# Three attention value blocks moved in TensorE's order, and smaller first loads of x, in a two-layer decoder trunk

## The chip, the cores and the metric

The kernel runs on one core of a Trainium2 chip. The metric is the device time of one execution in microseconds (us). A core has five engines with queues of their own: PE (TensorE, the matmuls; its weight loads appear as PEld), DVE (VectorE), ACT (ScalarE), POOL (GpSimd) and SP (SyncE, which here issues the DMAs). They wait for one another through semaphores.

## The reference

One sequence of 256 tokens, 1024 wide, goes through two layers and a last RMSNorm. In each layer three token mixers read the same normalised input, each is multiplied by a gate, and their sum goes through `w_out`; then comes an MLP with a squared ReLU.

```python
p = h @ w_in            # queries, keys, values and gates of all three mixers
merged = (sigmoid(g_mla)  * (o_mla  @ w_branch_mla)     # causal attention, 8 heads
        + sigmoid(g_moba) * (o_moba @ w_branch_moba)    # 256 tokens are one block: causal attention, 8 heads
        + sigmoid(g_ret)  * (o_ret  @ w_branch_ret))    # retention with decay, 4 heads
x = x + merged @ w_out
x = x + square(relu(h2 @ w_mlp_up)) @ w_mlp_down
```

An attention head computes scores `q k^T`, a softmax over the causal part, and `p v`, 64 wide ("values" below).

## The kernel before

**Numbers.** A matrix is split into a high and a low part, and a product is made of three matmuls (`three`, L228 to L230): high times high, low times high, high times low. Weights arrive by DMA (L192, tile `raw`), ACT makes the high part (`whi`, L207) and DVE the low one (`wlo`, L209).

**Stages of a layer.** Projections of the normalised input for MLA and MoBA; then, in program order, the MLA gate (gmla), the MoBA gate (gmoba), the MLA branch matmul (bmla), the projections for retention (rqk, rv, rg), the MoBA branch (bmoba), the retention gate and branch, `w_out` and the MLP. The list `prog` holds these units, and `at(slot, step)` hangs smaller steps behind one of them: scores, transposes, values, ropes.

**One attention.** `attention()` serves both. For each head: scores (MLA's in `mla_score`; MoBA's four heads at a time in `together`, L478), the row maximum on DVE (L492, L495), its negative times the scale on DVE (L498), the exponential on ACT (L501), the reciprocal of the sum (L504) and the division on DVE (two instructions of L506), three PE transposes into `ps_pt` (L512, `turned`) and a copy to `probT` by ACT. `values(h0)` multiplies the values of four heads: sixteen matmuls that use 64 columns of the array (L540 with 256 moving columns, L542 with 128) into a tile `po`, which ACT and DVE then split into high and low (L249; `omlah`, `omlal`, `omobah`, `omobal`).

**The order of the work.** A scheduler places each engine's instructions by a simulated timeline, so a step may come out later or earlier than written. Where the order is to be fixed, `in_a_row(...)` turns the scheduler off for PE: the matmuls of all its jobs stand one behind the other, and what the other engines do with them follows. The rows concerned:

- In MLA `values(0)` (heads 0 to 3) and `values(4)` are handed on (L551) to the row of MoBA's first four score heads (L563). In layer 0 the scheduler nevertheless put six full matmuls between the two blocks of values; in layer 1 they stand together. In the text "V" is a block of values, "S" the scores of four heads, "full matmul" one of L228 to L230 (128 x 512).
- MoBA's `values(0)` stand ahead of its second four score heads (L564), and `values(4)` behind retention's scores (L1051, tile `ps_r`, `moba_last`).
- `turned` of MoBA's heads is hung on later slots (L565 to L567).

**Rope.** In layer 0, four pairs of heads of MoBA are rotated on POOL (`rope_turned`, L443 and L446): a DMA swaps quarters of the partitions into `qkoth`, POOL multiplies that and the original by tables and adds them. For retention, DVE does it, with one product on POOL.

**First loads.** `begin` (L617 ff.) issues the first weight tiles, and x comes in eight chunks of 128 KB, one for each step k of the first projection (`start`, matmuls at L739 to L750): chunks 2 and 3 in one DMA, chunks 4 to 7 in another, among the weight tiles `b0mq` 1 to 7 of 464 KB each (L632 to L639).

Of the kernel before, what the change touches and what calls it, by code (L numbers as in the profile page):

```python
# [19 lines left out]
KD = D // P  # L20
# [117 lines left out]
def trunk(ctx: ExitStack, tc: tile.TileContext, gx, wts, consts, gfin, gn, xtok, out):  # L138


    nc = tc.nc
# [10 lines left out]
    X = [GX[:, G_END:].rearrange("p (k s) -> p k s", k=4), cp.tile([P, 4, S], F32, name="x1")]  # L152
    x = gx[:, G_END:].rearrange("p (k s) -> p k s", k=KD)
# [34 lines left out]
    def transfer(key, raw, queue=nc.sync, parts=None):  # L188
        offset, n, c = where[key]
        sz = n * c  # L190
        for a, b in parts or ((0, sz),):
            queue.dma_start(  # L192
                raw[:, a:b], bass.AP(tensor=wts.tensor, offset=wts.offset + offset + a, ap=[[sz, P], [1, b - a]])
            )
# [20 lines left out]
    def acc_tile(name="acc"):  # L215
        return ps.tile([P, 512], F32, name=name, tag="acc", bufs=4)

    def misc_tile(name="misc"):
        return ps.tile([P, 512], F32, name=name, tag="misc", bufs=4)
# [18 lines left out]
    def small(name):  # L238
        return sb.tile([P, 8], F32, name=name, tag="st", bufs=12)
# [8 lines left out]
    def split_plain(src, hi, lo):  # L248
        return nc.scalar.activation(hi, src, AF.Copy), nc.vector.tensor_sub(lo, src, hi.bitcast(F32))  # L249
# [212 lines left out]
    def in_a_row(*jobs):  # L462


        with tc.manual_schedule(engines={mybir.EngineType.PE}):
            rest = [job() for job in jobs]
        for job in rest:
            job()
# [11 lines left out]
    def attention_head(score, scale):  # L480


        got = {}

        def scores(s_ps=None):
            if s_ps is None:
                s_ps = misc_tile("ps_s")
                score(s_ps[:, 0:P], slice(0, P), slice(0, P))
                score(s_ps[:, P : 3 * P], slice(P, S), slice(0, S))
            p = sb.tile([P, 3 * P], F32, name="prob", bufs=4)  # L490
            m = small("smx")
            nc.vector.tensor_tensor_reduce(  # L492
                p[:, 0:P], s_ps[:, 0:P], mask[:, P : 2 * P], 1.0, NEG_INF, ALU.add, ALU.max, m[:, 0:1]
            )
            nc.vector.tensor_tensor_reduce(  # L495
                p[:, P : 3 * P], s_ps[:, P : 3 * P], mask, 1.0, NEG_INF, ALU.add, ALU.max, m[:, 1:2]
            )
            nc.vector.tensor_scalar(m[:, 2:4], m[:, 0:2], -scale, None, op0=ALU.mult)  # L498
            spans = ((0, P), (P, 3 * P))
            for i, (a, b) in enumerate(spans):  # L500
                nc.scalar.activation(  # L501
                    p[:, a:b], p[:, a:b], AF.Exp, bias=m[:, 2 + i : 3 + i], scale=scale, accum_out=m[:, 4 + i : 5 + i]
                )
            nc.vector.reciprocal(m[:, 6:8], m[:, 4:6])  # L504
            for i, (a, b) in enumerate(spans):
                nc.vector.tensor_scalar(p[:, a:b], p[:, a:b], m[:, 6 + i : 7 + i], None, op0=ALU.mult)  # L506
            got["p"] = p

        def turn():
            pt = misc_tile("ps_pt")  # L510
            for i, src in enumerate((0, P, 2 * P)):
                nc.tensor.transpose(pt[:, P * i : P * i + P], got["p"][:, src : src + P], ident)  # L512
            pT = sb.tile([P, 3 * P], F32, name="probT", bufs=8)
            nc.scalar.activation(pT, pt[:, : 3 * P], AF.Copy)
            return pT

        return scores, turn

    def attention(oT, score, vs, scale, first, group=None, former=None):

        pT = {}

        def turned(h, turn):
            pT[h] = turn()

        def values(h0):


            o, v = acc_tile("po"), vs()
            for h in (h0 + 2, h0):
                cs = slice(S * (h - h0) // 2, S * (h - h0) // 2 + S)
                for i in range(2):
                    for j in (1, 0):
                        vh = v[i][:, VD * (h + j) : VD * (h + j) + VD]
                        dst = o[64 * j : 64 * j + 64, cs]
                        if i == 0:
                            nc.tensor.matmul(dst, vh, pT[h + j][:, 0:S], start=True, stop=False)  # L540
                        else:
                            nc.tensor.matmul(dst[:, P:S], vh, pT[h + j][:, S : 3 * P], start=False, stop=True)  # L542
            dst = (part[:, h0 // 2 : h0 // 2 + 2, :].rearrange("p k s -> p (k s)") for part in oT)
            return lambda: split_plain(o, *dst)

        heads = [attention_head(lambda o, qs, ks, h=h: score(h, o, qs, ks), scale) for h in range(8)]
        if group is None:
            for h, (scores, turn) in enumerate(heads):
                at(first + h, scores)
                at(first + h + 2, lambda h=h, turn=turn: turned(h, turn))  # L550
            return [lambda: values(0), lambda: values(4)]  # L551

        def four(h0):
            banks = group(h0)

            def rest():
                for h, bank in enumerate(banks, h0):
                    heads[h][0](bank)

            return rest  # L560


        at(first, lambda: in_a_row(*former, lambda: four(0)))  # L563
        at(first + GAP, lambda: in_a_row(lambda: values(0), lambda: four(4)))  # L564
        for i in range(2):  # L565
            for h in range(4):
                at(first + GAP * i + 3 + h // 2, lambda h=4 * i + h: turned(h, heads[h][1]))  # L567
        return lambda: values(4)

    def gates(l, key, xn):  # L570

# [43 lines left out]
    def begin(key, tag=None, bufs=None, queue=nc.sync, parts=None):  # L615
        if tag:
            started[key] = sb.tile([P, 512 if tag == "w2k" else 1024], F32, name="raw0", tag=tag, bufs=bufs)  # L617
        else:
            started[key] = wp.tile([P, 1024], F32, name="raw", bufs=RAW)
        transfer(key, started[key], queue, parts)  # L620
# [8 lines left out]
    xn = Normed(G_ATT, 0)  # L629
    xrows = [w2k("xrow") for _ in range(2 * NT)]  # L630
    begin((0, "b0mq", 1), "t4", T4, parts=((0, 416), (416, 928)))
    nc.sync.dma_start(X[0][:, 2:4, :], x[:, 2:4, :])  # L632
    begin((0, "b0mq", 2), "t4", T4)
    begin((0, "b0mq", 3), "t4", T4)
    nc.sync.dma_start(X[1], x[:, 4:8, :])
    begin((0, "b0mq", 4), "t4", T4)
    for k in range(5, KD):
        begin((0, "b0mq", k))
    for q in range(2 * NT):  # L639
        nc.sync.dma_start(xrows[q], xtok[:, q // 2, 512 * (q % 2) : 512 * (q % 2) + 512])  # L640
    begin((0, "mk", 0, 0))
# [14 lines left out]
    def at(slot, step):  # L656
        steps.setdefault(slot, []).append(step)

    def slot(key, j):
        return [k for k, _ in prog].index((key, j))  # L660
# [9 lines left out]
    def layer(l, xn, before):  # L670
# [219 lines left out]
        first = slot("mv", 3)  # L890
        at(first, lambda: omlaT.extend((t4("omlah"), t4("omlal"))))

        def mla_score(h, o, qs, ks):
            nc.tensor.matmul(o, mla["Q"][:, h, qs], mla["K"][:, h, ks], start=True, stop=True)  # L894

        mla_last = attention(omlaT, mla_score, lambda: mla["v"], QKD**-0.5, first)


# [15 lines left out]
        first = slot("gmoba1", 1)  # L914
        at(first, lambda: omobaT.extend((t4("omobah"), t4("omobal"))))

        def moba_scores(h0):
# [5 lines left out]
            return banks  # L923

        moba_last = attention(omobaT, None, lambda: mqkv["mv"], MB_D**-0.5, first, moba_scores, mla_last)


# [14 lines left out]
        rT, or_ps, aT, rg, oret = [], [], {}, {}, []  # L942
# [105 lines left out]
                merged_turn(0, i - 1)  # L1048

        branch(l, "bret", oretT, th_ret, merged, between)  # L1050
        at(slot("rg", 1), lambda: in_a_row(ret_scores, moba_last))  # L1051
        for h in range(RT_H):
            at(slot("rg", 3), lambda h=h: ret_values(h))
        at(slot("rg", 3), group_norm)
# [218 lines left out]
    for l in range(L):  # L1273
        xn, before = layer(l, xn, before)
# [6 lines left out]
GAP = 8  # L1281
T4 = 8
# [81 lines left out]
```

## Time and profile before

| | |
|---|---|
| median of three runs | 833.33 us (833.25 to 833.34) |
| the profiled execution | 833.55 us |
| its span on the core | 831.8 us |
| DVE busy | 588.3 us (71%) |
| ACT busy | 484.1 us (58%) |
| POOL busy | 91.0 us (11%) |
| HBM read | 150.98 MB |

The span runs from the first instruction to the last; 833.55 - 831.8 = 1.75 us lie around it. In the timeline a row gives the start, the time from the first start to the last end, the engine, the line, the operation, output and inputs, the shape, and how many instructions it holds. Matmuls are pipelined, so their durations overlap: what counts on PE is the distance from one start to the next.

### The profile page before, as it was taken

What the parts mean: (1) busy time and instruction counts of PE and PEld (TensorE: products, weight loads), DVE (VectorE), ACT (ScalarE), POOL (GpSimd) and SP (SyncE); (2) the same over time, 40 slices, a digit from 0 to 9 for tenths busy, and PEclk for the clock granted to TensorE, in tenths of its full rate; (3) what the DMA queues carried; (4) which work ended last, traced back from release to release, by engine and by line L of the source; (5) the groups of instructions that cost most, each with busy time, mean ns of one, the idle gap of its engine ahead of it and who ended that gap; (6) DMA issues with size and microseconds to landing.
All of it is one profiled execution on the core that took longest, in us unless ns stands there. A gap on an engine that the chain in (4) does not pass through costs nothing.

```text
span 831.8 us, 12150 instructions
## 1 busy us (share of the span) xinstructions
PE 824.8 (99%) x4363; PEld 701.1 (84%) x4363; DVE 588.3 (71%) x1059; ACT 484.1 (58%) x861; POOL 91.0 (11%) x75
## 2 busy tenths in 40 slices
PE   9999999999999999999999999999999999999997
PEld 7888878888888888888898887888888888888886
DVE  6877887595787665656697976677868766556663
ACT  7677665445556555555686575654545555555552
POOL 0100440040030000000035210003100300000000
PEclk9999999999999999999999999999999999999999
DMA  9966664647457565665557657555565665666611
GB/s 346 342 217 192 196 197 151 202 131 222 138 187 229 185 196 186 196 188 175 179 181 215 198 167 253 153 154 175 155 201 157 213 188 182 196 203 184 195 53 50
DMA packets 46092, 156.49 MB, mean 188 GB/s; under 512 B 5840, under 2 KB 6864, under 8 KB 45776
## 3 DMA queue, kind: packets, MB, share of 16 engines
q1 hardware_dynamic: 45456, 155.05, 59.0%
q8 instruction: 34, 0.56, 0.3%
q10 hardware_dynamic: 576, 0.67, 0.2%
q14 instruction: 26, 0.21, 0.1%
HBM read 150.98 MB, written 1.05 MB: 183 GB/s over the span
## 4 chain that ended last, share of the span: by engine, by line
PE 98%; DVE 1%; ACT 0%; issue 0%; DVEq 0%
PE acc L228 18%; PE acc L229 18%; PE acc L230 18%; PE pup L1122 14%; PE pup L1124 7%; PE acc L1072 5%; PE acc L409 4%; PE acc L411 2%; PE ps_pt L512 1%; PE ps_s L894 1%; PE acc L739 1%; PE po L540 1%; PE ps_s L478 1%; PE warm L650 0%; PE acc L741 0%; PE po L542 0%
## 5 line engine op out<-in xcount | busy, mean ns | idle before, releaser
L209 DVE TENSOR_TENSOR wlo<-raw,whi 128x1024 fp32r<-128x1024 f32 (+4 forms) x287 | 345.5, 1212 | 176.5 <-ACT whi L207 117.4
L207 ACT ACTIVATE whi<-raw 128x1024 fp32r<-128x1024 f32 (+4 forms) x287 | 291.6, 1024 | 190.4 <-PE acc L230 101.7
L1122 PE MATMUL pup<-xs,whi 128*128 128x512 f32 x504 | 123.5, 390 | 0.0
L228 PE MATMUL acc<-whi,xs 128*128 128x512 f32 (+1 forms) x304 | 119.7, 395 | 0.0
L230 PE MATMUL acc<-whi,xs 128*128 128x512 f32 (+1 forms) x304 | 118.9, 391 | 0.0
L229 PE MATMUL acc<-wlo,xs 128*128 128x512 f32 (+1 forms) x304 | 118.6, 390 | 0.0
L1122 PEld LDWEIGHTS pup<-xs,whi 128*128 128x128 f32 x504 | 93.4, 188 | 18.6
L228 PE MATMUL acc<-whi,sq 128*128 128x512 f32 x256 | 100.1, 391 | 0.0
L229 PE MATMUL acc<-wlo,sq 128*128 128x512 f32 x256 | 99.9, 390 | 0.0
L230 PE MATMUL acc<-whi,sq 128*128 128x512 f32 x256 | 98.5, 389 | 0.0
L1124 PE MATMUL pup<-xs,wlo 128*128 128x256 f32 x504 | 69.5, 283 | 0.0
L1124 PEld LDWEIGHTS pup<-xs,wlo 128*128 128x128 f32 x504 | 66.6, 191 | 3.1
L228 PEld LDWEIGHTS acc<-whi,xs 128*128 128x128 f32 x304 | 57.0, 188 | 11.8 <-issue 1.2
L230 PEld LDWEIGHTS acc<-whi,xs 128*128 128x128 f32 x304 | 57.1, 188 | 11.3
L229 PEld LDWEIGHTS acc<-wlo,xs 128*128 128x128 f32 x304 | 57.2, 188 | 10.7
L230 PEld LDWEIGHTS acc<-whi,sq 128*128 128x128 f32 x256 | 48.0, 188 | 10.1
L1133 ACT ACTIVATE relu<-relu 128x256 f32<-128x256 f32 x64 | 25.5, 409 | 53.0 <-DVE relu L1132 53.0
L228 PEld LDWEIGHTS acc<-whi,sq 128*128 128x128 f32 x256 | 48.2, 188 | 9.2
L229 PEld LDWEIGHTS acc<-wlo,sq 128*128 128x128 f32 x256 | 48.2, 188 | 9.0
L285 POOL TENSOR_TENSOR sqsum<-sqsum,xsq 128x256 f32<-128x256 f32 x16 | 16.7, 1044 | 293.2 <-ACT xs L244 169.7
L501 ACT ACTIVATE prob<-prob,smx 128x128 f32<-128x128 f32 x64 | 28.4, 445 | 23.3 <-DVE smx L498 23.3
L409 PE MATMUL acc<-xs,whi 128*128 128x512 f32 x160 | 40.5, 395 | 0.0
(226 smaller groups left out, 1139.6 us busy)
## 6 DMA issues: line engine op xcount, KB each, us to landing
raw<-wts SPq DMA_DIRECT2D x264, 512.0 KB, 4.2
qkoth<-qkraw SPq DMA_DIRECT2D x48, 64.0 KB, 4.0
raw<-wts SPq DMA_DIRECT2D x6, 464.0 KB, 8.3
dec<-consts SPq DMA_DIRECT2D x2, 1024.0 KB, 7.1
raw<-wts SPq DMA_DIRECT2D x4, 416.0 KB, 3.2
xrow<-xtok SPq DMA_DIRECT2D x4, 256.0 KB, 8.1
gn<-gn SPq DMA_DIRECT2D x2, 512.0 KB, 9.1
raw<-wts SPq DMA_DIRECT2D x3, 256.0 KB, 3.8
```

The costliest lines, as they stand in the source:

```text
L207: nc.scalar.activation(hi[:, cs], raw[:, cs], AF.Copy)
L209: nc.vector.tensor_sub(lo[:, cs], raw[:, cs], hi[:, cs].bitcast(F32))
L228: nc.tensor.matmul(o, ah, bh, start=start, stop=False)
L229: nc.tensor.matmul(o, ah, bl, start=False, stop=False)
L230: nc.tensor.matmul(o, al, bh, start=False, stop=stop)
L285: (nc.gpsimd if n < self.on_pool else nc.vector).tensor_add(self.sum, self.sum, sq)
L409: nc.tensor.matmul(acc, wh[:, k, :], xn.both(k), start=k == 0, stop=False)
L501: nc.scalar.activation(p[:, a:b], p[:, a:b], AF.Exp, bias=m[:, 2 + i : 3 + i], scale=scale, accum_out=m[:, 4 + i : 5 + i])
L1072: nc.tensor.matmul(o, a, b, start=half == 0 and i == 0, stop=4 * half + n == KD and i == len(jobs) - 1)
L1122: nc.tensor.matmul(u, w, xm.both(k), start=k == 0, stop=False)
L1124: nc.tensor.matmul(u[:, 0:S], w, xm.k(k)[0], start=False, stop=k == KD - 1)
L1133: nc.scalar.activation(s, s, AF.Square)
```

## The change

1. In `attention()` the blocks are listed as `[values(4), values(0)]`. For MLA this list is handed on as it is, so heads 4 to 7 come in front of heads 0 to 3 in the row with MoBA's first scores.
2. For MoBA `values(0)` leaves the row of the second score heads, and both blocks, heads 0 to 3 first, follow retention's scores in one row.
3. Chunks 2 and 3 of x come in a DMA each, chunks 4 to 7 in two DMAs of two chunks, each just ahead of the weight tile of its step, and the weight tile of step 2 comes in two parts (416 and 512 columns). SP has three DMAs more.

In the order that the built program has, layer 0's row of V, V and S (now without the six full matmuls between) comes 18 full matmuls later than its first V did before. Behind it stand 27 full matmuls (before: 30), then the transposes of MoBA's heads 0 and 1 one behind the other, four full matmuls, those of head 2, one full matmul, those of head 3. Layer 1's row of MLA is unchanged but for the order of its two V. POOL's order is unchanged.

```diff
--- before.py
+++ after.py
@@ -520,7 +520,6 @@
 
 
 
-
         pT = {}
 
         def turned(h, turn):
@@ -543,12 +542,14 @@
             dst = (part[:, h0 // 2 : h0 // 2 + 2, :].rearrange("p k s -> p (k s)") for part in oT)
             return lambda: split_plain(o, *dst)
 
+
+        blocks = [lambda: values(4), lambda: values(0)]
         heads = [attention_head(lambda o, qs, ks, h=h: score(h, o, qs, ks), scale) for h in range(8)]
         if group is None:
             for h, (scores, turn) in enumerate(heads):
                 at(first + h, scores)
                 at(first + h + 2, lambda h=h, turn=turn: turned(h, turn))
-            return [lambda: values(0), lambda: values(4)]
+            return blocks
 
         def four(h0):
             banks = group(h0)
@@ -561,11 +562,11 @@
 
 
         at(first, lambda: in_a_row(*former, lambda: four(0)))
-        at(first + GAP, lambda: in_a_row(lambda: values(0), lambda: four(4)))
+        at(first + GAP, lambda: in_a_row(lambda: four(4)))
         for i in range(2):
             for h in range(4):
                 at(first + GAP * i + 3 + h // 2, lambda h=4 * i + h: turned(h, heads[h][1]))
-        return lambda: values(4)
+        return blocks[::-1]
 
     def gates(l, key, xn):
 
@@ -629,13 +630,16 @@
     xn = Normed(G_ATT, 0)
     xrows = [w2k("xrow") for _ in range(2 * NT)]
     begin((0, "b0mq", 1), "t4", T4, parts=((0, 416), (416, 928)))
-    nc.sync.dma_start(X[0][:, 2:4, :], x[:, 2:4, :])
-    begin((0, "b0mq", 2), "t4", T4)
-    begin((0, "b0mq", 3), "t4", T4)
-    nc.sync.dma_start(X[1], x[:, 4:8, :])
-    begin((0, "b0mq", 4), "t4", T4)
-    for k in range(5, KD):
-        begin((0, "b0mq", k))
+    for k in range(2, KD):
+
+        if k < 4:
+            nc.sync.dma_start(X[0][:, k, :], x[:, k, :])
+        elif k % 2 == 0:
+            nc.sync.dma_start(X[1][:, k - 4 : k - 2, :], x[:, k : k + 2, :])
+        if k < 5:
+            begin((0, "b0mq", k), "t4", T4, parts=((0, 416), (416, 928)) if k == 2 else None)
+        else:
+            begin((0, "b0mq", k))
     for q in range(2 * NT):
         nc.sync.dma_start(xrows[q], xtok[:, q // 2, 512 * (q % 2) : 512 * (q % 2) + 512])
     begin((0, "mk", 0, 0))
@@ -1048,7 +1052,7 @@
                 merged_turn(0, i - 1)
 
         branch(l, "bret", oretT, th_ret, merged, between)
-        at(slot("rg", 1), lambda: in_a_row(ret_scores, moba_last))
+        at(slot("rg", 1), lambda: in_a_row(ret_scores, *moba_last))
         for h in range(RT_H):
             at(slot("rg", 3), lambda h=h: ret_values(h))
         at(slot("rg", 3), group_norm)
```

## Prediction

> **What bounds the kernel now.** I read the page first, then PE's waits, then the timelines of PE, DVE and POOL around the places that the change touches.
>
> ```profile
> PE 824.8 (99%) x4363; PEld 701.1 (84%) x4363; DVE 588.3 (71%) x1059; ACT 484.1 (58%) x861; POOL 91.0 (11%) x75
> ...
> PEclk9999999999999999999999999999999999999999
> ```
> ```profile
> PE ps_pt L512 <- DVE prob L506: 0.2, 1, 0.2
> ```
>
> PE is busy 99% of the span at an undisturbed clock, and the list of its waits from 4 us on holds one entry: the transposes of the second MoBA head wait once for their softmax. So every edit is worth what it changes on PE: the distances between the starts of its matmuls where it changes over between kinds of matmul, and that one stall. What other engines gain counts nothing unless PE waits for it.
>
> **The values of MLA in layer 0.** Before, six full matmuls stand between the two blocks V. Layer 1 already has the row that layer 0 now gets, so its price can be read, not guessed. First layer 0, then layer 1:
>
> ```profile
> 101.78 0.39 PE L230 MATMUL acc<-whi,xs 128*128 128x512 f32 x1
> 102.09 0.65 PE L540 MATMUL po<-probT,vml 128*64 128x256 f32 x4
> ...
> 103.88 0.40 PE L229 MATMUL acc<-wlo,xs 128*128 128x512 f32 x1
> ...
> 104.81 0.40 PE L230 MATMUL acc<-whi,xs 128*128 128x512 f32 x1
> ...
> 108.10 0.50 PE L228 MATMUL acc<-whi,xs 128*128 128x512 f32 x1
> 108.44 0.39 PE L229 MATMUL acc<-wlo,xs 128*128 128x512 f32 x1
> ```
> ```profile
> 512.53 0.39 PE L230 MATMUL acc<-whi,xs 128*128 128x512 f32 x1
> 512.85 0.65 PE L540 MATMUL po<-probT,vml 128*64 128x256 f32 x4
> ...
> 514.20 0.60 PE L540 MATMUL po<-probT,vml 128*64 128x256 f32 x4
> ...
> 515.60 1.58 PE L478 MATMUL ps_s<-qkT 64*128 64x128 f32 x16
> 517.11 0.50 PE L228 MATMUL acc<-whi,xs 128*128 128x512 f32 x1
> 517.45 0.39 PE L229 MATMUL acc<-wlo,xs 128*128 128x512 f32 x1
> ```
>
> A full matmul that follows another starts 0.23 us later; each stretch below holds the first and the last such start, so two of them (0.46) are taken off. V alone: 103.88 - 101.78 - 0.46 = 1.64. V and S: 108.44 - 104.81 - 0.46 = 3.17. Together 4.81. In layer 1, V, V and S: 517.45 - 512.53 - 0.46 = 4.46. The difference, one change from full matmuls to V and back, is **0.35 us**. Layer 1's own MLA row only exchanges its two V: nothing.
>
> **MoBA's values(0), both layers.** They leave the place ahead of S and come behind retention's scores, beside the other V.
>
> ```profile
> 130.75 0.65 PE L540 MATMUL po<-probT,mv 128*64 128x256 f32 x4
> ...
> 132.20 1.58 PE L478 MATMUL ps_s<-qkT 64*128 64x128 f32 x16
> ```
>
> V between full matmuls and S took 132.20 - 130.75 = 1.45 us; the way into S afterwards costs what the way into V did. At the new place a second V follows a V. In layer 1's row above the first V took 514.20 - 512.85 = 1.35 with the way in and the second 515.60 - 514.20 = 1.40 with the way out; a V with both took 1.45, so one without either is 1.35 + 1.40 - 1.45 = 1.30 us. The move gives 1.45 - 1.30 = 0.15 us in each layer, **0.30 us** in all. The bounds: 0.05 each if the added V costs the 1.40 of one that has a way out, and 0.15.
>
> Later `omobah` and `omobal` for heads 0 to 3 cost nothing: the row hangs on the second of rg's four units, and the other two, 24 full matmuls or 24 x 0.23 = 5.5 us, cover their split before the MoBA branch. S of heads 4 to 7 comes earlier, and the transposes of these heads are spread by a few full matmuls. What could come late there is head 5, whose division stands on DVE behind a rope step that waits for POOL:
>
> ```profile
> 139.82 0.69 DVE L446 TENSOR_TENSOR qkT<-qkT,qkoth 128x512 f32<-128x512 f32 x1 [2.02 <-POOL qkoth L443]
> ```
> ```profile
> 142.16 0.82 PE L512 MATMUL ps_pt<-K,prob 128*128 128x128 f32 x6
> ```
>
> Even if the swap arrives no sooner than before, head 5 is divided by 139.82 + 0.69 + 0.55 (a pair of L506, below) = 141.1. PE's transposes of heads 4 and 5 stood at 142.16. They come earlier by V and by the gains in front of it, 1.45 + 0.35 + 0.54 = 2.34, so at 139.8 for head 4; in the new order nine full matmuls stand between it and head 5, which is due at 139.82 + 9 x 0.23 = 141.9. The cover is 0.8 us; what the swap is later than that, PE waits. I put nothing.
>
> **The stall.** In layer 0 the transposes of heads 0 and 1 of MoBA, and undisturbed ones to compare with:
>
> ```profile
> 115.04 0.49 PE L512 MATMUL ps_pt<-K,prob 128*128 128x128 f32 x3
> 115.71 0.70 PE L512 MATMUL ps_pt<-K,prob 128*128 128x128 f32 x3 [0.18 <-DVE prob L506]
> ...
> 116.48 0.40 PE L229 MATMUL acc<-wlo,omlah 128*128 128x512 f32 x1
> ...
> 118.98 0.82 PE L512 MATMUL ps_pt<-K,prob 128*128 128x128 f32 x6
> ...
> 119.88 0.39 PE L229 MATMUL acc<-wlo,omlah 128*128 128x512 f32 x1
> ```
>
> The six with the way back took 116.48 - 115.04 = 1.44 us, undisturbed 119.88 - 118.98 = 0.90: the stall costs **0.54 us**, more than the idle time of 0.18 that the row names. Why was head 1 late? DVE and POOL at that time:
>
> ```profile
> 109.05 0.16 DVE L498 TENSOR_SCALAR smx<-smx 128x2 f32<-128x2 f32 x1
> ...
> 111.67 1.25 DVE L498 TENSOR_SCALAR smx<-smx 128x2 f32<-128x2 f32 x1
> 112.84 1.59 DVE L506 TENSOR_SCALAR prob<-prob,smx 128x128 f32<-128x128 f32 x2
> ...
> 114.53 1.38 DVE L506 TENSOR_SCALAR prob<-prob,smx 128x128 f32<-128x128 f32 x2
> ...
> 116.02 0.55 DVE L506 TENSOR_SCALAR prob<-prob,smx 128x128 f32<-128x128 f32 x2
> ```
> ```profile
> 106.51 1.27 POOL L443 TENSOR_TENSOR qkoth<-qkoth,tab 128x512 f32<-128x512 f32 x1 [11.59 <-DVE omlal L249]
> ...
> 111.61 1.29 POOL L443 TENSOR_TENSOR qkT<-qkraw,tab 128x512 f32<-128x512 f32 x1
> 112.98 1.30 POOL L446 TENSOR_TENSOR qkT<-qkT,qkoth 128x512 f32<-128x512 f32 x1
> 114.23 1.34 POOL L420 TENSOR_TENSOR tab<-dec,rrow 128x512 f32<-128x512 f32 x1
> ```
>
> POOL works from 106.51 to 115.57 (114.23 + 1.34) on seven operations of about 1.3 us, one upon the other. Meanwhile L498 takes up to 1.25 us in place of 0.16 and a pair of L506 1.38 to 1.59 in place of 0.55, and they end close to where a POOL operation ends (112.92 and 112.98, 114.43 and 114.28); once POOL is done a pair takes 0.55 again. These steps of the softmax wait for POOL's operation to end.
>
> This decides the sum, since the row now comes later while POOL's work does not: its start hangs on DMAs of the swap that are issued in front. The new row starts 18 full matmuls after 102.09: 102.09 + 18 x 0.228 = 106.19. V, V and S as in layer 1 (517.11 - 512.85 = 4.26): S ends at 110.45, 2.35 later than before (108.10). DVE's first L498 falls due at 109.05 + 2.35 = 111.4 and meets POOL's operations at 111.61, 112.98, 114.23, 115.57: the four L498 end at about 111.7, 113.0, 114.3 and 115.6, with the maxima between them. Then POOL is quiet: the pair of head 0 runs to 116.2, that of head 1, behind its reciprocal, to 116.85. PE, from S's end: before, 30 full matmuls took 115.04 - 108.10 = 6.94; now 27, 0.68 less, so head 0's transposes are due at 116.71 and head 1's at 117.03. Both are ready, the second by 0.18 us only. I take the whole 0.54 as gone. Heads 2 and 3 are due at about 118.3 and 118.9 and ready at 117.6 and 118.3. The bounds: 0.54 gained, or 0.6 lost (rival 1).
>
> The Trainium skill ("SBUF — State Buffer", Who interferes with whom) has such a rule: VectorE and GpSimd share a pair of ports, one instruction holds it to its end, and the other blocks. By it the new softmax can't end before POOL's last boundary but runs freely after, which gives 832.1; without it, the chain keeping its old distance behind S, it is 833.2. The rows above agree with it, and no run of before shows the new position.
>
> The values' new order also makes heads 0 to 3 of `omlah` later. On DVE their split stands ahead of the maxima, so it is done before the first L498, at 111.4, and the MLA branch wants them after S and six full matmuls, at 110.45 + 0.11 + 6 x 0.23 = 111.9: covered by 0.5 us at least.
>
> **The first loads.** Fewer bytes now stand ahead of the weights of step 2, by 128 KB; all bytes are the same by step 7.
>
> ```profile
> 9.48 1.07 ACT L207 ACTIVATE whi<-raw 128x416 fp32r<-128x416 f32 x2 [1.89 <-DMA raw<-wts]
> ...
> 10.86 1.06 ACT L207 ACTIVATE whi<-raw 128x416 fp32r<-128x416 f32 x2
> ```
> ```profile
> 10.37 0.35 PE L747 MATMUL b<-whi,xs 128*128 128x416 f32 x1
> ...
> 12.92 0.36 PE L747 MATMUL b<-whi,xs 128*128 128x416 f32 x1
> ```
> ```profile
> 10.00:15.00 5.00, 5.00 (x30) 4.62 (x29) 4.93 (x11) 5.00 (x13) 0.00 (x0) 1.00 1.01 409
> ```
>
> ACT waits 1.89 us for step 2's weights, but PE doesn't: the first of the pair is split by about 10.03, and PE comes to it at 10.37. 128 KB at 409 GB/s is 0.32 us, which ACT gets and PE has no use for. Three more issues on SP stand where the DMA engines are already full (share 1.01). Worth: 0, hidden under PE's steps of 2.55 us.
>
> **The sum.** 0.35 + 0.30 + 0.54 = 1.19 us. The profiled execution (831.8 in the span and 1.75 around it) would become 833.55 - 1.19 = 832.36; the median, 0.22 under it, 833.33 - 1.19 = **832.1 us**. Two tenths of a per cent, 1.67 us, are about what a measurement of this kernel can tell from no change, so the forecast lies within them.
>
> **Rivals.**
>
> 1. *The softmax keeps its distance behind S, or meets one POOL operation more.* Before, head 1 was ready 115.71 - 108.10 = 7.61 us behind S; PE now wants it 117.03 - 110.45 = 6.58 behind: a stall of 1.03 (one POOL operation more gives 116.85 + 1.30 - 117.03 = 1.12). 832.14 + 1.03 = 833.2. For it: the margin is 0.18 us, less than the error of my placing. Against: POOL's chain is short of work at 115.57. Another operation on top, if the swap comes late, gives 834.5.
> 2. *Neighbours don't save a change,* because the scheduler's row is entered as dearly as before: 0.35 and 0.30 fall away, 832.14 + 0.65 = 832.8. Against it stands layer 1's row.
> 3. *Slower: the first loads starve PE.* A DMA of 128 KB took 3.1 us to land and one of 512 KB 7.3:
>
> ```profile
> x<-gx SPq DMA_DIRECT2D x1, 512.0 KB, 7.3
> ...
> raw<-wts SPq DMA_DIRECT2D x1, 128.0 KB, 3.1
> ```
>
>    A line through both leaves 1.7 us that don't depend on the size. Were each added DMA to cost that in series, step 2 would come 1.7 - 0.32 = 1.4 later against 0.34 of slack, step 3 3.4 later against 12.92 - 11.4 = 1.5, step 4 5.1 later against 1.8 (by the same steps): a stall of 3.3 in all, 832.14 + 3.3 = 835.4. It decides from 0.66 us a transfer at step 2 and beats the gain from about 1.0. Against it: with a share of 1.01 the fixed part overlaps with other transfers.
> 4. *More is gained than I see,* over 1.67 us: no row points to it.
>
> **How the numbers follow.** The forecast 52% (own range 831.8 to 832.5, from the bounds of the two values and a rest of the stall), rival 1 24% and with the second operation 4%, rival 2 8%, rival 3 7%, rival 4 5%. The range 831.7 to 833.7 takes in the forecast, 1 at 833.2 and 2: 84%. Faster by over 0.2% is rival 4, 5%; slower rival 3, 7%; the rest, 88%, lies within.
>
> **What would show it.** PE's waits after: no `ps_pt` entry, or one of about 0.1 us (forecast); one near 117 behind DVE's L506 (rival 1). In layer 0's timeline: V to V 1.35, V to S 1.40; behind `ps_r` 1.35 and 1.40 in both layers. L498 should end at POOL's boundaries near 111.6, 113.0, 114.3, 115.6. At the start, ACT's wait of 1.89 shrinks by some 0.3, and PE has no idle row before 26 us; an idle row at L747 is rival 3. Wrong would be the whole if PE, with the same neighbours, starts its matmuls at other distances than these.

## The result and the profile after

| | before | changed |
|---|---|---|
| median of 21 runs each | 833.41 us (832.97 to 833.89) | 832.29 us (831.66 to 832.97) |
| the profiled execution | 833.55 us | 832.71 us |
| its span | 831.8 us | 830.9 us |

The ratio is 0.9986, with a 95% interval of 0.9980 to 0.9992: 1.12 us less, by the interval 0.7 to 1.7 us. The two profiled executions differ by 0.84 us.

The page's first part and the list of PE's waits from 4 us on, after the change (the list has its heading only):

```profile
PE 824.3 (99%) x4363; PEld 701.2 (84%) x4363; DVE 588.2 (71%) x1059; ACT 484.1 (58%) x861; POOL 92.0 (11%) x75
```
```profile
engine line waited for: us in total, times, longest us
```

PE is as busy as before, and the one wait is gone from the list. PE's timeline after, layer 0 (start, time to the last end, engine, line, tiles): the row of V, V and S, then the transposes of heads 0 and 1 with the way back:

```profile
105.93 0.39 PE L230 MATMUL acc<-whi,xs 128*128 128x512 f32 x1
106.25 0.65 PE L539 MATMUL po<-probT,vml 128*64 128x256 f32 x4
...
107.60 0.60 PE L539 MATMUL po<-probT,vml 128*64 128x256 f32 x4
...
109.00 1.58 PE L478 MATMUL ps_s<-qkT 64*128 64x128 f32 x16
110.51 0.50 PE L228 MATMUL acc<-whi,xs 128*128 128x512 f32 x1
110.84 0.39 PE L229 MATMUL acc<-wlo,xs 128*128 128x512 f32 x1
...
116.77 1.09 PE L512 MATMUL ps_pt<-K,prob 128*128 128x128 f32 x6
...
117.93 0.39 PE L229 MATMUL acc<-wlo,omlah 128*128 128x512 f32 x1
```

The row takes 110.84 - 105.93 - 0.46 = 4.45 us, and V follows V after 1.35, as forecast. The transposes take 117.93 - 116.77 = 1.16 us with the way back, though no wait is listed: 1.44 before, 0.90 undisturbed. So of the stall of 0.54 us, 0.26 are left. A wait can show in the starts alone.

MoBA's two V behind retention's scores, layer 0:

```profile
156.77 0.65 PE L539 MATMUL po<-probT,mv 128*64 128x256 f32 x4
...
158.12 0.60 PE L539 MATMUL po<-probT,mv 128*64 128x256 f32 x4
...
159.52 0.50 PE L228 MATMUL acc<-whi,xs 128*128 128x512 f32 x1
```

Two V take 159.52 - 156.77 = 2.75 us, 1.30 more than one with both its ways (1.45): again as forecast.

Where both kernels have done the same work up to a matmul, its two starts can be compared directly. The table does so at five places of the profiled executions, and at the end of the span:

| place | before | changed | difference |
|---|---|---|---|
| ahead of MLA's row, layer 0 | 98.11 | 98.16 | +0.05 |
| behind the transposes of heads 0 to 3 | 122.38 | 121.84 | -0.54 |
| behind MoBA's values, layer 0 | 160.16 | 159.52 | -0.64 |
| behind MoBA's values, layer 1 | 569.99 | 569.28 | -0.71 |
| the last matmul | 825.36 | 824.65 | -0.71 |
| end of the span | 831.8 | 830.9 | -0.89 (before rounding) |

MLA's row and the stall thus gave 0.59 us. That is 0.05 less than the 0.36 and 0.28 read from the rows; the difference builds up over the full matmuls behind the transposes of heads 2 and 3, which now stand apart. MoBA's move gave 0.10 and 0.07 us, 0.17 in both layers, where 0.30 was forecast. The last 0.18 us lie behind the last matmul, where the forecast had no term. There SP waits for one semaphore after the other until every DMA has landed (its EVENT_SEMAPHORE rows, with the start of the first and of the last). Before, then changed:

```profile
825.36 0.39 PE L230 MATMUL acc<-whi,sq 128*128 128x512 f32 x1
```
```profile
L1360 SPq EVENT_SEMAPHORE  x7: 17/28/28, 830.5 to 831.7; - x7
```
```profile
824.65 0.39 PE L230 MATMUL acc<-whi,sq 128*128 128x512 f32 x1
```
```profile
L1364 SPq EVENT_SEMAPHORE  x7: 17/28/28, 827.7 to 830.8; - x7
```

In the trace of before, the two DMAs that store y signal the semaphores 104 and 105, the first two in SP's order: SP stands at the first until 830.5 and has the other waits, 0.06 us each, still to do. In the changed kernel they signal 108 and 109, three places further on, and the three waits ahead of these are done from 827.7 on, while the data still moves. The three DMAs more at the start would move them by three; that this is how the numbers are given out is my reading, the places and times are the traces'.

### The profile page after: what moved, and what is told of

It is laid out like the page before. It is cut to its first block, busy times and chain, and to the rows that moved or that the text cites. A ratio compares the mean times of both kernels' runs of the same rounds, so it can differ in the third digit from the quotient of the medians.

```text
span 830.9 us, 12159 instructions
## 1 busy us (share of the span) xinstructions
PE 824.3 (99%) x4363; PEld 701.2 (84%) x4363; DVE 588.2 (71%) x1059; ACT 484.1 (58%) x861; POOL 92.0 (11%) x75
## 4 chain that ended last, share of the span: by engine, by line
PE 99%; DVE 0%; ACT 0%; issue 0%; DVEq 0%
PE acc L228 18%; PE acc L229 18%; PE acc L230 18%; PE pup L1126 14%; PE pup L1128 7%; PE acc L1076 5%; PE acc L409 4%; PE acc L411 2%; PE ps_pt L512 1%; PE ps_s L898 1%; PE acc L743 1%; PE po L539 1%; PE ps_s L478 1%; PE warm L654 0%; PE acc L745 0%; PE pmt L1042 0%
```

## The experiments

Each kernel was timed in eleven runs beside the kernel before on the same chip; a profile shows one execution. With intervals of about 0.1% either way, the timings tell 1 us from 0, and the finer parts are read from the traces.

**MLA's order alone** (`e1_mla_only`).

```diff
-            return [lambda: values(0), lambda: values(4)]
+            return [lambda: values(4), lambda: values(0)]
```

> Only the order of MLA's two value blocks is changed (heads 4 to 7 first); PE's order in layer 0's MLA row is then that of the changed kernel, MoBA and the loads of x are as before. Theory (the gain is what PE's changes between kinds of matmul and the stall make it): 0.35 us from the row and about 0.27 of the stall's 0.54, 0.62 us in all, a ratio of 0.9993; the row V, V, S takes 4.46 us beside full matmuls, and the six transposes of heads 0 and 1 with the way back about 1.16 us in place of 1.44. Rival (POOL's rope starts at a fixed time, as the prediction had it): the six take 0.90, the gain is 0.89 us.

832.76 us against 833.49, ratio 0.9990 (0.9981 to 0.9999). In its trace the start is 0.13 us later than in that of before, the stretch from 98 us to the matmul behind the transposes of heads 0 to 3 gains 0.59, as in the changed kernel, and behind it there is no difference. The transposes, and POOL's first rope operation with the DVE instruction beside it:

```profile
116.85 1.10 PE L512 MATMUL ps_pt<-K,prob 128*128 128x128 f32 x6
...
118.02 0.39 PE L229 MATMUL acc<-wlo,omlah 128*128 128x512 f32 x1
```
```profile
106.55 2.03 POOL L443 TENSOR_TENSOR qkoth<-qkoth,tab 128x512 f32<-128x512 f32 x1 [11.54 <-DMA qkoth<-qkraw]
```
```profile
106.22 1.22 DVE L209 TENSOR_TENSOR wlo<-raw,whi 128x1024 fp32r<-128x1024 f32 x1 [0.53 <-DMA qkoth<-qkraw]
```

1.17 us: the theory's 1.16, not the rival's 0.90. POOL's work does not stand still when PE's row moves.

**MoBA's values alone** (`e2_moba_only`).

```diff
-        at(first + GAP, lambda: in_a_row(lambda: values(0), lambda: four(4)))
+        at(first + GAP, lambda: in_a_row(lambda: four(4)))
...
-        return lambda: values(4)
+        return [lambda: values(0), lambda: values(4)]
...
-        at(slot("rg", 1), lambda: in_a_row(ret_scores, moba_last))
+        at(slot("rg", 1), lambda: in_a_row(ret_scores, *moba_last))
```

> Only MoBA's values of heads 0 to 3 go behind retention's scores, in both layers. Theory: 0.15 us a layer for one way in and out, less some 0.01 us for each extra place at which transposes are now set among full matmuls: 0.2 to 0.3 us in all, ratio 0.9997; the stall of layer 0 stays (six transposes with the way back 1.44 us). Rival (the move costs, since the softmax of heads 4 to 7 comes earlier and meets POOL's rope): PE waits for head 5 behind 139.8, and nothing or less is gained.

833.60 us against 833.49, ratio 0.9999 (0.9990 to 1.0007): nothing that a timing shows. By starts compared as above, the move gives 0.07 us in each layer, less than the 0.10 to 0.15 that the theory had. No wait for head 5 appears, so the rival falls. The stall in layer 0, in front of everything that this edit moves, was larger in this execution:

```profile
115.28 0.27 PE L512 MATMUL ps_pt<-K,prob 128*128 128x128 f32 x1
...
117.08 0.40 PE L229 MATMUL acc<-wlo,omlah 128*128 128x512 f32 x1
```

1.80 us with the way back, 0.90 lost, where the theory had 1.44.

**The first loads alone** (`e3_x_only`), the third part of the change by itself:

```diff
-    nc.sync.dma_start(X[0][:, 2:4, :], x[:, 2:4, :])
-    begin((0, "b0mq", 2), "t4", T4)
...
+            nc.sync.dma_start(X[0][:, k, :], x[:, k, :])
...
+            begin((0, "b0mq", k), "t4", T4, parts=((0, 416), (416, 928)) if k == 2 else None)
```

> Only the first loads of x and of step 2's weights are cut smaller; PE's order is that of before to the last matmul. Theory: 0.0 us, ratio 1.0000; step 2's weights land earlier on ACT's side by over 1 us, and PE has no use for it. Rival (three more DMAs cost each its fixed part): PE idle at steps 2 to 4, up to 3.3 us slower.

833.50 us against 833.49, ratio 0.9998 (0.9989 to 1.0007). PE's list of waits has the old entry for `ps_pt` alone. ACT's timeline there:

```profile
8.16 1.26 ACT L207 ACTIVATE whi<-raw 128x416 fp32r<-128x416 f32 x2
...
10.37 1.07 ACT L207 ACTIVATE whi<-raw 128x416 fp32r<-128x416 f32 x2 [0.56 <-DMA raw<-wts]
```

Step 2's weights are split from 8.16 on, where it was 9.48, and the wait of 1.89 us is gone. The second row is step 3, split from 10.37 on behind a wait of 0.56 (10.86 before); PE comes to it at 12.83. PE makes nothing of either: from 6 to 100 us its starts keep the same distance of 0.08 to 0.09 us to those of before. The rival, starving loads, falls here.

Behind PE's last matmul these loads do gain. From its start to the end of the span it is 6.22 to 6.23 us in the four kernels with the new loads (changed, e3, e4, e5) and 6.38 to 6.40 in the five with the old ones (before, e1, e2, e6, e7): 0.16 to 0.18 us that the theory of 0.0 did not have, too little for the timings to show.

**Rope later** (`e4_late_rope`), the changed kernel with

```diff
-            for i, (key, j) in enumerate((("gmoba0", 0), ("gmoba0", 1), ("gmoba1", 0), ("gmoba1", 1))):
+            for i, (key, j) in enumerate((("gmoba0", 0), ("gmoba0", 1), ("bmla0", 0), ("bmla0", 1))):
```

> The changed kernel, with the partition swap of MoBA's second pairs in layer 0 issued behind five weight loads, so that POOL's six rope operations come after the softmax of heads 0 to 3; the orders of PE, DVE, ACT and POOL stay. Theory (DVE's L498 and L506 wait for POOL's operation to end): L498 takes 0.16 us, a pair of L506 0.55, and the six transposes with the way back 0.90 in place of 1.16, so 0.26 us under the changed kernel, ratio to before 0.9983. Rival (the softmax is late for another reason, such as its own length behind the scores): L506 of head 1 ends as late as in the changed kernel, at 117.3, and no time is gained. Second rival (the swap comes too late for the scores of heads 4 to 7 at 130.2): PE stalls there by what the rope ends later.

833.22 us against 833.49, ratio 0.9999 (0.9990 to 1.0008). POOL, DVE and PE in its trace:

```profile
114.20 1.29 POOL L443 TENSOR_TENSOR qkoth<-qkoth,tab 128x512 f32<-128x512 f32 x1 [19.57 <-DMA qkoth<-qkraw]
```
```profile
111.78 0.16 DVE L498 TENSOR_SCALAR smx<-smx 128x2 f32<-128x2 f32 x1
...
117.01 2.50 DVE L506 TENSOR_SCALAR prob<-prob,smx 128x128 f32<-128x128 f32 x2
```
```profile
116.46 0.82 PE L512 MATMUL ps_pt<-K,prob 128*128 128x128 f32 x6
...
117.36 0.39 PE L229 MATMUL acc<-wlo,omlah 128*128 128x512 f32 x1
...
119.57 0.44 PE L512 MATMUL ps_pt<-K,prob 128*128 128x128 f32 x2 [0.67 <-DVE prob L506]
...
143.14 0.33 PE L512 MATMUL ps_pt<-K,prob 128*128 128x128 f32 x1 [0.56 <-DVE prob L506]
```

The mechanism is as the theory has it: with POOL quiet L498 takes 0.16 us and the six transposes 117.36 - 116.46 = 0.90. The gain is not: heads 2 and 3 now meet POOL's rope (a pair of L506 takes 2.50 us), and PE waits 0.67 us for head 3. It waits 0.56 more for head 5: the next swap, retention's, landed later in this kernel (at 140.38; 137.47 in the changed one), and DVE's order puts the divisions of heads 5 to 7 behind the rope step that needs it. The second rival named the wrong place, but its kind came true: a swap that is too late.

**Rope earlier** (`e5_gn_late`), the changed kernel with the load of retention's norm weights behind the swap; SP's order is the only one that changes:

```diff
-        at(slot("rqk", 0), load_gn)
+        at(slot("rqk", 2), load_gn)
```

> The changed kernel, with the 512 KB load of retention's norm weights issued behind the partition swap of MoBA's second pairs (it stood ahead of it); the orders of PE, DVE, ACT and POOL stay. Theory (POOL's rope sets when the softmax steps of heads 0 and 1 end, and the swap's landing sets when POOL starts): the swap lands some 1.25 us earlier, POOL starts at about 105.1 instead of 106.3 and ends at about 114.3 to 115.0 instead of 116.2, so head 1 is ready before 117.0 and the six transposes with the way back take 0.90 us instead of 1.16: 0.26 us under the changed kernel, ratio to before 0.9983. Rival (the stall hangs on the distance behind the scores): still 1.16. Second rival (POOL's first operation meets another DVE instruction, as it met the weight split at 106.1): POOL ends no earlier.

832.04 us against 833.54, ratio 0.9982 (0.9973 to 0.9991), the fastest of all. Its POOL, DVE and PE:

```profile
104.93 1.71 POOL L443 TENSOR_TENSOR qkoth<-qkoth,tab 128x512 f32<-128x512 f32 x1 [10.12 <-DMA qkoth<-qkraw]
106.60 2.26 POOL L443 TENSOR_TENSOR qkT<-qkraw,tab 128x512 f32<-128x512 f32 x1
...
114.05 1.29 POOL L420 TENSOR_TENSOR tab<-dec,rrow 128x512 f32<-128x512 f32 x1
```
```profile
105.86 1.86 DVE L209 TENSOR_TENSOR wlo<-raw,whi 128x1024 fp32r<-128x1024 f32 x1 [0.37 <-ACT whi L207]
...
115.93 0.55 DVE L506 TENSOR_SCALAR prob<-prob,smx 128x128 f32<-128x128 f32 x2
```
```profile
116.49 0.82 PE L512 MATMUL ps_pt<-K,prob 128*128 128x128 f32 x6
...
117.38 0.39 PE L229 MATMUL acc<-wlo,omlah 128*128 128x512 f32 x1
```

The swap lets POOL start at 104.93. Its first two operations meet DVE's weight splits (1.71 and 2.26 us in place of 1.27), which the second rival foresaw, yet it ends at 115.34, 0.9 sooner than in the changed kernel. Head 1 is divided from 115.93 and the transposes take 0.89: no stall. From 98 us to the matmul behind the transposes of heads 0 to 3 it gains 0.83 us against before; the changed kernel gained 0.59. Its median is 0.25 us under that of the changed kernel; the timings can't separate the two, the traces do.

**The same in the kernel before** (`e6_before_gn_late`).

> The kernel before with the same one load put behind the swap; the orders of PE, DVE, ACT and POOL stay. Theory: POOL's rope ends some 1.25 us earlier, at about 114.3, the pair of divisions of head 1 runs from about 114.5 to 115.1 and PE, which wants it at 115.26, does not wait: 0.5 us gained, ratio 0.9994, with none of the change in it. Rival: the six transposes still take over 1.4 us with the way back.

833.07 us against 833.54, ratio 0.9993 (0.9984 to 1.0002). The stall is gone here too, with nothing of the change in it:

```profile
115.15 0.82 PE L512 MATMUL ps_pt<-K,prob 128*128 128x128 f32 x6
...
116.04 0.39 PE L229 MATMUL acc<-wlo,omlah 128*128 128x512 f32 x1
```

0.89 us in place of 1.44, and 0.55 gained against before over the same stretch. The interval of the timing includes no change; the trace shows the gain.

**The change without the loads of x** (`e7_no_x`): the changed kernel with the old lines L632 to L639.

> The changed kernel with the first loads of x and of step 2's weights as before; PE's order is that of the changed kernel. Theory: the same time as the changed kernel (ratio to before 0.9987, PE's row 4.46, transposes 1.16). Rival (part of the gain is the earlier first weights): about 0.3 us slower than the changed kernel, with PE idle before 13 us.

832.33 us against 833.54, ratio 0.9986 (0.9978 to 0.9995), where the changed kernel has 832.29 and 0.9986. The row and the transposes are those of the changed kernel:

```profile
116.29 1.09 PE L512 MATMUL ps_pt<-K,prob 128*128 128x128 f32 x6
...
117.45 0.40 PE L229 MATMUL acc<-wlo,omlah 128*128 128x512 f32 x1
```

PE idles once for 0.23 us, before its very first weight matmul, ahead of the loads that the edit touches. A second loss shows in the starts alone, at step 2's weights:

```profile
9.22 0.63 PE L742 MATMUL acc<-xs,wlo 128*128 128x256 f32 x4
9.83 0.45 PE L748 MATMUL b<-whi,xs 128*128 128x416 f32 x1
10.12 0.35 PE L749 MATMUL b<-whi,xs 128*128 128x416 f32 x1
```

These two distances, 0.61 and 0.29 us, were 0.48 and 0.18 before: PE had come 0.67 us sooner in this execution and lost 0.24 of it to the old loads. In e4, with the new loads, PE came 0.58 sooner and lost 0.31 at step 1. Which loads cost PE less over many executions is not shown by these single traces.

## Why the prediction held, step by step

1. **MLA's row, 0.35 us: right.** 4.81 became 4.45, by 0.36. Reading the price from layer 1, which already had the row, was exact.
2. **MoBA's move, 0.30 us: the mechanism right, the size about half (0.17, and 0.13 in e2).** The way in and out saves 0.15 a layer as worked out (V behind V adds 1.30). What I put at nothing was the spreading of the transposes. The way from the first transpose of head 4 to the second full matmul behind the last one of head 7, in layer 0, before (its start, 142.16, stands in the prediction) and changed; both hold twelve transposes and thirteen full matmuls:

```profile
146.45 0.39 PE L229 MATMUL acc<-wlo,xs 128*128 128x512 f32 x1
```
```profile
140.17 0.49 PE L512 MATMUL ps_pt<-K,prob 128*128 128x128 f32 x3
...
142.12 0.27 PE L512 MATMUL ps_pt<-K,prob 128*128 128x128 f32 x1
...
142.47 0.38 PE L512 MATMUL ps_pt<-K,prob 128*128 128x128 f32 x2
...
144.51 0.39 PE L229 MATMUL acc<-wlo,xs 128*128 128x512 f32 x1
```

   146.45 - 142.16 = 4.29 us became 144.51 - 140.17 = 4.34; over the longer way from S to the last transposes, in layer 1, the loss is 0.07. That is the part that was missing. The forecast named the regrouping and gave it no price. The waits that I feared there (head 5) did not come, though seven full matmuls, not the nine that I counted, stand between the transposes of heads 4 and 5.
3. **The stall, 0.54 us: the mechanism right, half of the size.** The step that failed is "while POOL's work does not", the sentence that held POOL's rope fixed. POOL and DVE in the changed kernel:

```profile
106.31 2.19 POOL L443 TENSOR_TENSOR qkoth<-qkoth,tab 128x512 f32<-128x512 f32 x1 [11.53 <-DMA qkoth<-qkraw]
...
114.94 1.29 POOL L420 TENSOR_TENSOR tab<-dec,rrow 128x512 f32<-128x512 f32 x1
```
```profile
106.14 1.22 DVE L209 TENSOR_TENSOR wlo<-raw,whi 128x1024 fp32r<-128x1024 f32 x1 [0.66 <-DMA qkoth<-qkraw]
...
114.99 1.26 DVE L498 TENSOR_SCALAR smx<-smx 128x2 f32<-128x2 f32 x1
...
116.82 0.55 DVE L506 TENSOR_SCALAR prob<-prob,smx 128x128 f32<-128x128 f32 x2
```

   With the values moved back, a weight split comes on DVE at 106.14, and POOL's first operation takes 2.19 us in place of 1.27: it ends 1.14 after the split does (108.50 and 107.36), about the time that it takes alone. The chain then ends at 116.23, not 115.57. Each L498 still ends close to a boundary of POOL's, the last at 116.25, the pair of head 1 at 117.37 instead of 116.85; PE wanted it at 117.1, and the margin of 0.18 that I had was used up. So the wait goes both ways between the two engines; I had used one direction only. The Trainium skill ("SBUF — State Buffer", Who interferes with whom) has both: whichever instruction issues first holds the shared ports for its whole length, and the other is blocked. e5 and e6, which move nothing but one DMA, show that POOL's rope and not the distance behind S sets the stall, and in e4, with POOL quiet, it is gone too. Rival 1 had the right place, and a quarter of its price came true: 0.26 of 1.03.
4. **The first loads, nothing: right for PE in e3, wrong for the kernel.** ACT's wait for step 2 shrank not by 0.3 but went; the smaller first part can be split before the second lands, which the 128 KB alone don't give. PE made nothing of it in e3. What the forecast left out is the end of the kernel: the three DMAs more bring 0.18 us there.

The traces' terms, 0.59 for the row and the stall, 0.17 and 0.18, make 0.94 us (the span has 0.89, as the changed execution began 0.05 later), against 1.19 forecast and 1.12 measured. That the forecast came this close is in part luck: the 0.18 at the end, which it did not have, made up for some of what it had too much in the stall and in MoBA's move. The rest, 0.94 against 1.12, is within the interval of 0.7 to 1.7. One source of it can be seen: the stall in kernels with PE's old order up to there is 0.54 in the trace of before, 0.90 in e2, and in e3

```profile
114.95 0.27 PE L512 MATMUL ps_pt<-K,prob 128*128 128x128 f32 x1
...
116.55 0.40 PE L229 MATMUL acc<-wlo,omlah 128*128 128x512 f32 x1
```

1.60 - 0.90 = 0.70. If 0.7 is nearer to its mean, the change took some 0.2 more from it than the trace of before says; one execution each can't settle that, and it stays open.

## What to carry to other kernels

On an engine that is never idle, price a reorder by the distances between starts where the kind of instruction changes, and look for the same neighbours elsewhere in the trace: they are the measurement. Compare both traces at matmuls that have the same work behind them, and go on past the last one: a part of the gain can lie outside the places that an edit was meant for. A chain on another engine that seems fixed in time is fixed only as long as what runs beside it stays; list what the reorder brings next to its first instruction. When two engines hold each other up, moving one DMA ahead of a large one that nobody needs yet can be worth as much as reordering the work.

## What the runs showed of the hardware

- DVE and GpSimd hold each other up here until the other's instruction ends: a 128x2 operation of 0.16 us took 1.26 beside a 128x512 GpSimd operation in the changed kernel (1.31 in e2), that one 2.19 instead of 1.27 beside a DVE subtraction of 128x1024, and in e5 a DVE split took 1.86 instead of 1.22. Not every DVE operation is held up: the masked maximum L492, which reads the scores from PSUM, kept its 0.28 to 0.29 us throughout.
- The waits of SP at the end of the kernel take 0.06 us each. Whether the DMAs that store y stand early or late in their order was worth 0.16 to 0.18 us in these nine traces.
- The first steps scatter whatever the loads are: up to 60 us the executions differ by -0.42 (e7) to +0.25 us (e2) from that of before, a good part of the scatter of a single run.
